# Fetching and putting back the expert rows of a mixture-of-experts layer by a fixed number for each place, instead of by whole groups of 32

## The chip, the cores and the metric

The kernel runs on one core of one Trainium2 chip. The metric is device time in microseconds (us), lower is better. The engines are named as in the profile: PE is TensorE (PEld its weight loads), DVE is VectorE, ACT is ScalarE, POOL is GpSimd, SP is SyncE. The core's 16 DMA engines move all data between HBM and the on-chip memory, whichever engine issues the transfer.

## The reference, cut to what matters

One layer over 512 tokens of width 1024: adaLN, a projection, a convolution and attention, and then a mixture of experts in float32. A router gives each token four of 32 experts; each expert multiplies its tokens' rows by a 1024 x 2048 and a 1024 x 1024 matrix.

```python
def moe_ffn(h, w_router, b_router, w_gate_up, b_gate_up, w_down, b_down):
    logits = jnp.dot(h, w_router, preferred_element_type=jnp.float32) + b_router.astype(jnp.float32)
    top_logit, top_idx = lax.top_k(logits, TOP_K)
    gate = jax.nn.softmax(top_logit, axis=-1)
...
    def expert_block(args):
        tok, g, e = args
        xb = h_pad[tok]
        gu = xb @ w_gate_up[e] + b_gate_up[e]
        y = clamped_swiglu(gu) @ w_down[e] + b_down[e]
        return y * g[:, None].astype(y.dtype)
...
    out = jnp.zeros((n_tok + 1, d), y.dtype).at[slot_tok].add(y.reshape(n_slots, d))
```

There are 512 x 4 = 2048 pairs of token and expert. How many fall to each expert depends on the data.

## The kernel before, in words

The first 330 us or so are the dense part (adaLN, projections, attention, convolution, output projection, router). The rest is the experts.

**Places.** The kernel counts the tokens of each expert on the chip and sorts the experts by count (`sort`). Expert 0 always has place 0; the others have places 1 to 31, by falling count. The numbers of slots are fixed for each place: 128 for places 0 to 3, 96 for places 4 to 15, 64 for places 16 to 31, that is `groups(i)` groups of `W = 32`, 2688 slots in all. `idx` holds, for each place, the token of each slot; an empty slot points to a spare row of its own, past the 512 tokens. Tokens that find no slot go to an `overflow` branch, which loads the weights of their expert once more. With the counts that the reference's inputs give (seeds 0 to 3), no expert has more tokens than its place has slots.

**Order of work.** The places are worked off in the order of `place(i)`, i from 0 to 31: a place of the upper half (four or three groups, called heavy here) and one of the lower half (two groups, light) in turn. For each expert there are eight loads of 1 MB for the first product and four for the second. `fetch` issues them from SP, in one order written out ahead (`seq`), into a ring of 1 MB buffers: 13, and 6 more from the sixth product of expert 0 on. A load waits until PE has read its buffer, and until the load eight places ahead, whose semaphore it takes over, has landed; so at most eight loads are under way.

**Rows.** `gather(i)` (POOL, an indirect DMA from the DRAM table `H2` into `xg`) fetches n rows of 4 KB, one a partition; `turn_x(i)` transposes them on PE. `gather(i + 2)` is issued as soon as `turn_x(i + 1)` has freed `xg`. `put_back(i)` weighs the products on DVE into `y`, and `scatter` (POOL, an indirect DMA) adds the n rows of `y` to the DRAM table `ACC`. Place 0 isn't fetched (it is built on the chip) and place 31 isn't put back (its rows are added on the chip), so 31 transfers of either kind run. The matrix products always work on whole groups.

## Time and profile before

| | us |
|---|---|
| time, median of 3 runs (1430.43 to 1435.80) | 1435.26 |
| the profiled execution: its own time | 1430.19 |
| its span, first to last instruction | 1428.5 |
| PE busy with matmuls | 1303.4 |
| DVE busy | 470.3 |
| POOL busy | 193.4 |

The profiled execution's time is its span and 1.7 us around it. It is as fast as the fastest of the three runs and 5.1 us under their median. A busy PE is not a PE at its peak: matmul records overlap and their ends are modelled.

### The profile page before, as it was taken

The numbers are of one execution on the slowest core, as the hardware profiler recorded it, in microseconds if no ns is written. First come the engines' busy times: TensorE is split into PE (matmuls) and PEld (weight loads), VectorE is DVE, ScalarE is ACT, GpSimd is POOL, SyncE is SP. The second block draws the span as 40 slices with busy tenths as digits, with TensorE's granted clock in tenths as the row PEclk, the third lists the DMA queues.
The fourth block names the chain that finished last, engine by engine and source line by source line (L and its number), as shares of the span: only waits on it lengthen the run. The fifth ranks groups of instructions, "written<-read, shape, count | busy, mean of one in ns | idle before, by whom it ended". The sixth has DMA issues, their size and how long they took to land.

```text
span 1428.5 us, 29373 instructions
## 1 busy us (share of the span) xinstructions
PE 1303.4 (91%) x12798; PEld 645.1 (45%) x12798; DVE 470.3 (33%) x954; ACT 227.7 (16%) x362; POOL 193.4 (14%) x152
## 2 busy tenths in 40 slices
PE   5799879998899999999989899998989899989894
PEld 1577768784444343444434333433333344434341
DVE  2787655546122331222222121322121222131224
ACT  1425555432000010000000000000000000000002
POOL 0421632212002100000010000010000000000102
PEclk9899999999999999999999999999999999999997
DMA  9446524237999999999999999999999999999994
GB/s 351 165 156 228 206 91 165 99 125 289 378 381 372 394 399 399 397 402 396 402 397 399 393 414 395 407 380 391 401 395 412 396 399 394 397 395 392 397 393 183
DMA packets 79486, 483.05 MB, mean 338 GB/s; under 512 B 9725, under 2 KB 10553, under 8 KB 27129
## 3 DMA queue, kind: packets, MB, share of 16 engines
q1 hardware_dynamic: 71298, 453.58, 79.7%
q0 software_dynamic: 7952, 27.53, 7.3%
q8 instruction: 102, 1.67, 0.5%
q14 instruction: 30, 0.25, 0.0%
q10 hardware_dynamic: 104, 0.03, 0.0%
HBM read 463.01 MB, written 18.09 MB: 337 GB/s over the span
## 4 chain that ended last, share of the span: by engine, by line
DMA 36%; PE 34%; issue 2%; DVE 1%; ACT 1%; ACTq 0%; SPq 0%; DVEq 0%
DMA raw<-in_w_gate_up_dram 19%; PE R L1013 11%; PE S L1013 9%; DMA hl<-in_w_gate_up_dram 8%; PE J L1013 7%; DMA hl<-in_w_down_dram 6%; DMA raw<-in_w_down_dram 3%; PE V L1013 3%; PE S L1256 1%; PE S L1027 1%; PE T L1220 1%; PE V L1038 1%; ACT aT L1267 0%; PE R L1027 0%; PE T L1256 0%
## 5 line engine op out<-in xcount | busy, mean ns | idle before, releaser
L1013 PE MATMUL S<-raw,xT 128*32 128x512 f32 x1440 | 174.3, 601 | 15.6 <-DMA raw<-in_w_gate_up_dram 13.9
L1013 PE MATMUL J<-raw,xT 128*32 128x512 f32 x1424 | 165.0, 595 | 7.5 <-DMA raw<-in_w_gate_up_dram 7.2
L1286 DVE SCALAR_TENSOR_TENSOR y<-R,gates,gt2r 32x256 f32<-32x256 f32 x208 | 99.9, 480 | 209.5 <-PE R L1013 206.7
L1270 POOL DMA_INDIRECT ACC<-y,idx x31 | 45.3, 1463 | 798.8 <-DVE selx L1060 798.8
L1286 DVE SCALAR_TENSOR_TENSOR y<-V,gates,gt2r 32x256 f32<-32x256 f32 x120 | 57.5, 479 | 240.6 <-PE V L1013 239.1
L1225 ACT ACTIVATE xT<-T 128x512 f32<-128x512 f32 (+1 forms) x31 | 18.2, 587 | 640.4 <-PE T L1220 599.9
L1013 PE MATMUL R<-raw,aT 128*32 128x256 f32 x2144 | 118.0, 379 | 2.4 <-DMA raw<-in_w_down_dram 2.4
L1013 PE MATMUL R<-raw,xT 128*32 128x512 f32 x896 | 114.1, 598 | 0.0
L1013 PEld LDWEIGHTS R<-raw,aT 128*32 128x32 f32 x2144 | 74.5, 110 | 48.9 <-PE J L1013 6.8
L1013 PEld LDWEIGHTS S<-raw,xT 128*32 128x32 f32 x1440 | 42.4, 110 | 107.5 <-issue 69.9
L1013 PEld LDWEIGHTS J<-raw,xT 128*32 128x32 f32 x1424 | 41.6, 109 | 101.4 <-issue 73.7
L1013 PE MATMUL V<-raw,aT 128*32 128x256 f32 x1280 | 73.6, 380 | 5.9 <-DMA raw<-in_w_down_dram 5.8
L1013 PE MATMUL S<-hl,xT 128*32 128x512 f32 x608 | 72.7, 595 | 6.8 <-DMA hl<-in_w_gate_up_dram 6.8
L1013 PE MATMUL J<-hl,xT 128*32 128x512 f32 x624 | 73.4, 596 | 4.4 <-DMA hl<-in_w_gate_up_dram 4.3
L1237 DVE TENSOR_SCALAR lm<-S 128x512 f32<-128x512 f32 x16 | 11.1, 692 | 196.7 <-ACT sg L1236 196.7
L1013 PE MATMUL R<-hl,aT 128*32 128x256 f32 x1184 | 67.7, 386 | 1.4 <-DMA hl<-in_w_down_dram 1.4
L1013 PEld LDWEIGHTS R<-raw,xT 128*32 128x32 f32 x896 | 30.8, 112 | 67.3 <-issue 67.2
L1013 PEld LDWEIGHTS V<-raw,aT 128*32 128x32 f32 x1280 | 40.2, 110 | 41.7 <-DMA raw<-in_w_down_dram 12.4
L1013 PEld LDWEIGHTS R<-hl,aT 128*32 128x32 f32 x1184 | 39.5, 112 | 29.7 <-issue 4.2
L1206 POOL DMA_INDIRECT xg<-H,idx x31 | 29.2, 942 | 156.0 <-PE T L1220 87.5
L1013 PE MATMUL R<-hl,xT 128*32 128x512 f32 x384 | 48.3, 592 | 0.0
L519 POOL TENSOR_TENSOR acc<-acc,raw 128x2048 f32<-128x2048 f32 x8 | 37.4, 4669 | 51.3 <-ACT raw L518 51.2
(489 smaller groups left out, 1603.5 us busy)
## 6 DMA issues: line engine op xcount, KB each, us to landing
raw<-in_w_gate_up_dram SPq DMA_DIRECT2D x179, 1024.0 KB
raw<-in_w_down_dram SPq DMA_DIRECT2D x85, 1024.0 KB
hl<-in_w_gate_up_dram SPq DMA_DIRECT2D x77, 1024.0 KB
hl<-in_w_down_dram SPq DMA_DIRECT2D x43, 1024.0 KB
raw<-in_w_ada_dram SPq DMA_DIRECT2D x24, 1024.0 KB
raw<-in_w_in_dram SPq DMA_DIRECT2D x10, 1024.0 KB
raw<-in_w_out_dram SPq DMA_DIRECT2D x4, 1024.0 KB
H<-t POOLq DMA_DIRECT2D x5, 512.0 KB, 3.2
```

Of the source, the lines that this page charges most:

```text
L519: G.tensor_add(v, v, t)
L1013: T.matmul(o(g)[j * W:(j + 1) * W], lhs(g), w(j), start=start and g % per == 0, stop=stop and (g % per == per - 1 or g == n - 1), skip_gro ...
L1027: T.matmul(a[g // 2][:, g % 2, :], selx[:, 2 * h:2 * h + 2, :].rearrange("p a c -> p (a c)"), bias[:, h * 512:(h + 1) * 512], start=False, ...
L1038: T.matmul(dn[i][n * HALF:(n + 1) * HALF, :], aT[i][:, r * 4 + j, :], w[:, r * D + n * 512:r * D + (n + 1) * 512], start=start, stop=stop)
L1206: G.indirect_dma_start(out=t, out_offset=None, in_=H2[:, :], in_offset=bass.IndirectOffsetOnAxis(ap=idx[0:n, q:q + 1], axis=0))
L1220: T.transpose(p_[:, c0:c0 + n], t[:, k * P:(k + 1) * P], ident[0:n, 0:n])
L1225: S.activation(d_, p_[:, 0:len(ks) * n], AF.Copy)
L1237: V.tensor_scalar(lv, u, LIMIT + 1.0, 1.0 - LIMIT, op0=OP.min, op1=OP.max)
L1256: T.transpose(p_[:, (2 * g + r) * P:(2 * g + r + 1) * P], r_[:, g * 256 + r:g * 256 + 256:2], ident)
L1270: G.indirect_dma_start(out=to, out_offset=bass.IndirectOffsetOnAxis(ap=ix_, axis=0), in_=y, in_offset=None, compute_op=OP.add)
L1286: V.scalar_tensor_tensor(y[g * W:(g + 1) * W, cs], quarter(a, g)[ps], gates4[ps, g, q:q + 1], gt2r[ps, cs], op0=OP.mult, op1=OP.mult)
```

## The change

`ROWS` gives a number of rows for each place, at most the slots that the place had: 2396 in all instead of 2688. `gather` and `scatter` move that many rows. The products, the transposes and the weighing still work on the whole groups, so the rows of `xg` past the fetched ones must hold something finite: `xg` becomes one tile (`xrows`) that is cleared once and then used by all gathers. The test for overflow now compares a count with `ROWS`: a table `less` (128 less the rows, by place) is filled by 23 memsets on POOL at the start, and one more DVE instruction behind the sort picks each expert's value. The last place's 512 gate columns, `gt2l`, move into `xrows`. With the reference's inputs (seeds 0 to 3) no count is over its place's new number, so the overflow branch stays untaken.

```diff
+ROWS = (128, 128, 112, 104, 96, 94, 90, 86, 84, 82, 80, 78, 78, 76, 75, 72,
+        64, 64, 64, 62, 62, 60, 60, 58, 58, 56, 56, 56, 55, 48, 46, 64)
...
     places()
+    for q in range(E):
+        if q == 0 or ROWS[q] != ROWS[q - 1]:
+            G.memset(less[:, q:E], float(P - ROWS[q]))
...
+        V.scalar_tensor_tensor(junk_[0:E, :], perm[0:E, 0, :], 1.0, less[0:E, :], op0=OP.mult, op1=OP.mult,
+                               accum_out=less_of)
...
-            V.tensor_copy(nb[:, 0:1], cnt[0:E, :])
-            for s in STEPS:
-                V.tensor_scalar(nb[:, 1:2], at[0:E, :], float(s), float(W), op0=OP.is_ge, op1=OP.mult)
-                V.tensor_add(nb[:, 0:1], nb[:, 0:1], nb[:, 1:2])
+            V.tensor_add(nb[:, 0:1], cnt[0:E, :], less_of)
...
     def gather(i):
-        n = groups(i) * W
-        t = m2.tile([n, D], F32, name="xg")
         q = place(i)
-        G.indirect_dma_start(out=t, out_offset=None, in_=H2[:, :],
+        n = ROWS[q]
+        t = xrows
+        G.indirect_dma_start(out=t[0:n, :], out_offset=None, in_=H2[:, :],
                              in_offset=bass.IndirectOffsetOnAxis(ap=idx[0:n, q:q + 1], axis=0))
...
-        q, a, n = place(i), dn.pop(i), groups(i) * W
-        y = m1.tile([n, D], F32, name="y", bufs=2)
+        q, a, n = place(i), dn.pop(i), ROWS[place(i)]
+        y = m1.tile([groups(i) * W, D], F32, name="y", bufs=2)
...
-        scatter(y, idx[0:n, q:q + 1])
+        scatter(y[0:n, :], idx[0:n, q:q + 1])
...
+    xrows = m2.tile([P, D], F32, name="xg")
+    V.memset(xrows, 0.0)
     gather(1)
```

The order of the transfers does not change; their sizes do. On POOL, from the third gather on (`xg<-H` is a gather, `ACC<-y` a scatter; 640 is the table's height), there stood before:

```order
L1206 DMA xg<-H_804,idx 96x1024
L1270 DMA ACC<-y,idx 640x1024
L1206 DMA xg<-H_804,idx 64x1024
L1270 DMA ACC<-y,idx 640x1024
L1206 DMA xg<-H_804,idx 96x1024
L1270 DMA ACC<-y,idx 640x1024
L1206 DMA xg<-H_804,idx 64x1024
L1270 DMA ACC<-y,idx 640x1024
L1206 DMA xg<-H_804,idx 128x1024
```

And in the same place now:

```order
L1213 DMA xg<-H_828,idx 94x1024
L1277 DMA ACC<-y,idx 640x1024
L1213 DMA xg<-H_828,idx 64x1024
L1277 DMA ACC<-y,idx 640x1024
L1213 DMA xg<-H_828,idx 90x1024
L1277 DMA ACC<-y,idx 640x1024
L1213 DMA xg<-H_828,idx 62x1024
L1277 DMA ACC<-y,idx 640x1024
L1213 DMA xg<-H_828,idx 128x1024
```

Before, every transfer had 64, 96 or 128 rows; now only places 1, 4, 16, 17, 18 and 31 keep their number, and most new numbers are no multiple of 16. SP's queue is the same, row for row. At the program's start POOL gets the memsets ahead of the clearing of `c64`, the left operand of the first products (`c_183`); these are the last six of them:

```order
L323 MEMSET less 128x9
L323 MEMSET less 128x7
L323 MEMSET less 128x4
L323 MEMSET less 128x3
L323 MEMSET less 128x2
L323 MEMSET less 128x1
L364 MEMSET c_183 128x512
L365 COPY c_183<-sl 128x8x2
```

Before, the memset of `c64` followed that of `ones_bf` at once. All but the first of the 23 wait for the one ahead, as they overlap.

## Rows read from the trace of the kernel before

**Rows 1.** The page: span; DMA share in 40 slices, in tenths.

```profile
span 1428.5 us, 29373 instructions
DMA  9446524237999999999999999999999999999994
```

**Rows 2.** Chain that ended last, 330 to 1429 us: start, us, what.

```profile
604.40 6.91 PE V L1013 x128
...
642.21 21.33 DMA raw<-in_w_down_dram
663.66 23.65 DMA raw<-in_w_gate_up_dram
...
1351.18 20.83 DMA hl<-in_w_down_dram
```

**Rows 3.** Windows: length, busy PE, PEld, DVE, ACT, POOL, granted clock, DMA share, GB/s.

```profile
440.00:640.00 200.00, 197.01 (x2225) 82.43 (x2221) 49.31 (x97) 15.53 (x27) 18.91 (x18) 1.00 1.02 392
640.00:1380.00 740.00, 687.89 (x7863) 285.39 (x7859) 167.87 (x342) 44.18 (x79) 51.83 (x43) 1.00 1.02 398
```

**Rows 4.** SP's waits, 740 to 1040 us: total us, times, longest.

```profile
SPq L128 <- DMA raw<-in_w_gate_up_dram: 115.8, 49, 4.7
...
SPq L128 <- PE R L1013: 4.2, 13, 0.4
```

**Rows 5.** DMA, 740 to 1040 us: packets, MB, share of 16 engines' time.

```profile
DMA packets 17336, 119.59 MB, mean 399 GB/s; under 512 B 2011, under 2 KB 2011, under 8 KB 3515
...
q1 hardware_dynamic: 15514, 112.98, 92.8%
q0 software_dynamic: 1792, 6.16, 8.3%
```

**Rows 6.** DMA, 497 to 504 us, a scatter of 64 rows.

```profile
q1 hardware_dynamic: 338, 2.44, 83.8%
q0 software_dynamic: 80, 0.26, 18.8%
```

**Rows 7.** DMA, 504 to 512 us, a gather of 96 rows.

```profile
q0 software_dynamic: 112, 0.39, 15.3%
```

**Rows 8.** DMA, 563 to 570 us, a gather of 128 rows.

```profile
q0 software_dynamic: 144, 0.52, 18.3%
```

**Rows 9.** Timeline of POOL: start, us, idle before. Gathers of i = 1, 4, 6.

```profile
362.71 0.98 POOL L1206 DMA_INDIRECT xg<-H,idx  x1 [16.04 <-issue]
452.05 0.96 POOL L1206 DMA_INDIRECT xg<-H,idx  x1
501.32 0.93 POOL L1206 DMA_INDIRECT xg<-H,idx  x1 [5.49 <-PE T L1220]
```

**Rows 10.** Timeline of PE: transposes of the same rows, i = 4, 6.

```profile
470.66 0.63 PE L1220 MATMUL T<-ident,xg 96*128 96x96 f32 x5
529.87 0.63 PE L1220 MATMUL T<-ident,xg 96*128 96x96 f32 x5
```

**Rows 11.** Tile `xg`: the transposes (ns min/median/max, first and last start); the gathers' landing.

```profile
L1220 PE MATMUL T<-ident,xg x200: 222/223/329, 391.0 to 1362.0; 64*128 64x64 f32 x64, 96*128 96x96 f32 x30, 128*128 128x128 f32 x6
...
DMA to landing us min/median/max: 7.8/9.1/12.2
```

**Rows 12.** Timelines of POOL and PE at the start.

```profile
0.38 0.10 POOL L1556 MEMSET const-float32-0.0<- 128x1 f32 x1 [0.38 <-issue]
...
5.02 0.20 POOL L359 COPY c<-sl 128x16 f32<-128x16 f32 x1 [2.80 <-DVE sl L355]
...
6.64 1.93 PE L378 MATMUL S<-raw,c 128*32 128x512 f32 x8 [3.82 <-DMA raw<-in_w_ada_dram]
```

**Rows 13.** Timeline of DVE, the sort and what follows.

```profile
336.99 0.17 DVE L1071 SCALAR_TENSOR_TENSOR kj<-T,own 64x32 f32<-64x32 f32 x1
...
352.47 1.28 DVE L1132 SCALAR_TENSOR_TENSOR bias<-y,sgn 128x1024 fp32r<-128x1024 f32 x1 [1.12 <-ACT y L1131]
...
378.56 0.69 DVE L1237 TENSOR_SCALAR lm<-S 128x512 f32<-128x512 f32 x1 [18.80 <-ACT sg L1236]
```

## The prediction

> **What bounds the kernel now.** I read the page first. The 16 DMA engines are idle for a good part of the dense stage and busy to nine tenths or more in every slice from 357 us to the tail [rows 1]. Then the chain: up to 640 us it consists of PE's products, from 642 us to 1372 us of transfers, nearly without a break [rows 2]. The windows say the same: from 440 to 640 us PE is busy for 197 of 200 us, from 640 to 1380 us for 688 of 740, so it stands still for 52 us there. The granted clock is 1.00 in both, the upper of its two levels, and the DMA share is 1.02 in both [rows 3]. SP's waits show why the transfers don't run ahead: between 740 and 1040 us SP waits 115.8 us for the landing of earlier loads into the first product's buffers alone, and 4.2 us for PE to give a buffer back [rows 4]. So the eight loads under way are the limit, and the DMA engines are full all the time. What is taken from their work after 440 us shortens the end by as much, as long as that is less than the 52 us that PE has to spare.

> **What a row costs.** The gathers and scatters are queue q0, the weights q1. Between 740 and 1040 us q0 has 1792 packets: 9 gathers and 9 scatters with 16 small ones each (288), and 1504 rows. Its share is 8.3% of 16 x 300 us, so 398 us, or 0.265 us of one engine for a row [rows 5]. The kinds differ. A scatter of 64 rows takes 18.8% of 16 x 7 us, which is 21.1 us or 0.329 us a row [rows 6]; a gather of 96 rows 15.3% of 16 x 8 us, 19.6 us or 0.204 us a row [rows 7]; a gather of 128 rows 18.3% of 16 x 7 us, 20.5 us or 0.160 us a row [rows 8]. So the gather of 128 rows costs hardly more than that of 96: where the rows lie on the partitions matters, not only how many they are. I take 0.204 for all gathers that are not of 128 rows.

> **What is saved.** 31 gathers fetch 2560 rows before and 2268 after, 31 scatters put back 2624 and 2332: 292 fewer of each. The first places (16, 4, 17) keep their rows, so all of it falls after 440 us. Scatters: 292 x 0.329 = 96.1 us. Gathers: 252 of the rows belong to places that had 96 or 64, 252 x 0.204 = 51.4 us; places 2 and 3 go from 128 rows to 112 and 104, and so from 2 x 20.5 us to 216 x 0.204 = 44.1 us, 3.1 us more. In all 144.4 us of one engine.

> What that is worth depends on how the rows are dealt out to the engines. Every transfer of before has a multiple of 16 rows, so no row here shows what happens with 94, 62 or 55. From both sides:
> - The rows are dealt out evenly, whatever their number: 144.4 / 16 = 9.0 us. (By q0's mean, 584 x 0.265 / 16 = 9.7 us; by bytes alone, 2.39 MB at the window's 398 GB/s, 6.0 us.)
> - All 16 engines take blocks, and the number is rounded up: an engine has n / 16 rows, rounded up. Every load of weights needs all 16 engines, so the fullest one counts, and it is always the same. It saves a row only at places 2, 3, 10 to 15, 29 and 30, ten in each direction: scatters 10 x 0.329 = 3.3 us; gathers 8 x 0.204 less 2 x 0.15 (8 rows at 0.160 become 7 at 0.204), 1.3 us; in all 4.6 us.

> That the price of a gathered row depends on the number of rows speaks for blocks of neighbouring partitions for each engine, so I take 4.6 us, and keep 9.7 as the other end.

> **What is added.**
> - 23 memsets on POOL at the start. A small one takes 0.10 us [rows 12]; as each waits for the one ahead I allow up to 0.19, 2.3 to 4.4 us. The copy of the conditioning vector into `c64` stands behind them; it ran at 5.02 us after 2.80 us of idleness, and the first product that reads it began at 6.64 us, when its weights had landed [rows 12]. So POOL, free for the copy from 2.2 us before, is free from 4.5 to 6.6 us now; copy and product begin at most about 0.4 us late. I take 0.2. Without that idle time it would be the whole 4.4.
> - One DVE instruction behind the sort, on the way to the table of experts that SP waits for: the nearest one took 0.17 us [rows 13]. In front of the overflow test four small ones go. I take 0.2.
> - Clearing `xrows`: up to 1.3 us, from the widest DVE instruction near it [rows 13]. DVE stands idle for 18.8 us ahead of its next work [rows 13], so nothing behind it waits, but the first gather now waits for it. It was issued at 362.7 us [rows 9], lands within 12.2 us, and is first read at 391.0 [rows 11]: nothing. Without that cover, 1.3 us.

> The products, transposes and weighing don't change. One tile for all gathers instead of a new one each time changes no wait: the next gather waited before, too, until PE had read the last [rows 9, 10].

> **Sum.** 4.6 saved, 0.4 added: 4.2 us less. On the profiled execution, 1430.19 us, that is 1426.0. The median of the runs lies 5.07 us above that execution; a difference carries over, so I forecast 1435.3 - 4.2 = 1431 us, with a range of its own of 1425 (9.7 saved) to 1435 (nothing saved but the added 0.4 hidden).

> **Rivals.**

> *Few engines per transfer (slower).* A block split needs not be rounded up: the transfer could be given to as many engines as divide its number of rows, at most 16. All of before are multiples of 16, and their 16 small packets per transfer [rows 5] fit this as well. Then 94, 90 and 62 rows go to 2, 15 and 2 engines. Two engines serve places 5, 7, 9, 19, 20, 23, 24 and 30 (548 rows), both ways. The work is no more than in the even case, but one engine of such a pair gets 274 x (0.204 + 0.329) = 146 us over 16 transfers, or 18.3 us for each of the 16 engines on the average. The loads of weights run at the pace of the engine that is furthest behind; eight loads under way, 8.4 MB at 398 GB/s, let the others run ahead by 21 us and no more. If the pairs come round evenly, the fullest is over the mean by about one large scatter, 47 x 0.329 - 2 = 13 us; if each transfer begins at the engine after the last one's, the ones with 15 and 14 engines move the start back by one or two, and the put back rows of experts 9, 10 and 14 and the fetched ones of 14 and 15 meet on one engine: (31 + 43 + 41) x 0.329 + (41 + 29) x 0.204 = 52 us, 34 over the mean. So 9.0 less and 13 to 34 more: 1440 to 1460, and I take 1450. It costs more than it saves as soon as one engine is over the mean by 9 us. A second effect speaks for slower as well: the gather for i = 4 has only 18.6 us from its issue to its first transpose, where that for i = 6 has 28.6 [rows 9, 10]. Landing takes 9.1 us in the middle [rows 11] with six rows an engine; 41 more at 0.204 and, if the two queues take turns, a packet of weights between each (83.8% of 112 us over 2.44 MB of 8 KB packets, 0.315 us [rows 6]) make it 30 us, so PE would stand for about 12 us at 470 us. PE is 197 of 200 us busy there; but the DMA engines go on loading meanwhile, into buffers that are free.

> [...]

> *An even deal.* As above, 9.0 saved and 0.4 added: 1426.7 us. For it: nothing obliges a list of rows to be cut in blocks. Against it: the gather's price by number of rows.

> *Hidden anyway.* If PE were the bound over the whole expert stage, nothing would come of it: 1435 us. The chain speaks against it from 642 us on [rows 2], and PE's 52 idle us [rows 3].

> **How the numbers follow.** Chances: all 16 engines with rounding up (the forecast) 0.33 and evenly 0.20, together the likelier kind; few engines 0.42; hidden 0.05. About 0.5%, 7.2 us, is what a measurement of this kernel can tell from no change. Faster by more: 0.65 of the even deal, a quarter of the forecast's case, little of the others, 0.24. Slower by more: most of the few engines' case, 0.38. Within: 0.38. The range reaches down to the even deal with its upper price and 2 us for the spread of the runs, 1423, and up to 1458, which leaves out the last part of the few engines' case.

> **What would show it.** q0's packets fall by 584, and its share between 740 and 1040 us by about a tenth, in every case. Right: the gathers' median landing stays within 1 us of 9.1, rates in the windows stay near 398 GB/s, and the last load lands some 4 us earlier. Wrong: landings of 20 us and more for 94, 86 and 82 rows, rates that fall under 390 GB/s after 640 us, and PE waiting there for more than 52 us. If the chain in the middle turns into PE, the hidden case holds.

## The result, and the profile after

The changed kernel takes 1472.88 us (median of 4 runs, 1470.36 to 1477.46) against 1432.85 us before (4 runs); the ratio is 1.0268, 95% interval 1.0242 to 1.0295. With fewer rows it is 40 us slower. The forecast was 1431 us with a range up to 1458.

From the page of the kernel after (span; DMA share in 40 slices; queues with packets, MB, share of 16 engines' time):

```profile
span 1472.1 us, 29396 instructions
DMA  8445544148999999999998999999999999999983
q1 hardware_dynamic: 71298, 453.58, 78.9%
q0 software_dynamic: 15824, 25.19, 6.8%
```

And the two queues on the page of the kernel before:

```profile
q1 hardware_dynamic: 71298, 453.58, 79.7%
q0 software_dynamic: 7952, 27.53, 7.3%
```

q0 moved fewer bytes, but its packets doubled. Its engine time fell from 7.3% of 1428.5 us, 104.3 us, to 6.8% of 1472.1, 100.1 us. The weights on q1, the same packets and bytes as before, went from 79.7% or 1138.5 us to 78.9% or 1161.5 us: 23 us more. (A share is rounded to 0.1%, so each of these is good to 0.7 us.) Together the DMA engines have 18.8 us more to do, and the span is 43.6 us longer; the other 25 us the engines stood idle. (The profiled execution of before is one of the fast ones, so the spans lie a little further apart than the medians.)

Where they stood idle the windows show (length, busy PE, PEld, DVE, ACT, POOL, granted clock, DMA share, GB/s):

```profile
440.00:640.00 200.00, 175.94 (x1968) 73.48 (x1964) 41.78 (x83) 13.14 (x23) 22.46 (x22) 0.93 1.01 384
640.00:1380.00 740.00, 689.67 (x7760) 285.11 (x7756) 168.65 (x342) 43.36 (x77) 60.84 (x44) 0.99 1.00 381
...
640.00:740.00 100.00, 98.50 (x1160) 42.13 (x1156) 23.99 (x48) 6.25 (x11) 9.33 (x6) 1.00 1.02 388
740.00:840.00 100.00, 87.70 (x956) 34.69 (x948) 22.38 (x46) 5.62 (x10) 9.09 (x6) 0.96 0.93 335
```

Before, the share was 1.02 and the rate 392 and 398 GB/s [rows 3]; now it is 381 GB/s after 640 us, and 335 at a share of 0.93 in the worst stretch, 740 to 840 us. The mean granted clock fell to 0.93 between 440 and 640 us, where PE was busy for 176 us instead of 197. That is a mean of two levels, 1.00 and 0.50: in windows of 2 us the clock is 1.00 up to 476 us, 0.50 from 478 to 486 and 1.00 again from 488, and 0.50 from 578 to 592 us, each time after PE had stopped for rows that had not landed (no product runs from 476 to 482 and from 576 to 586 us). Between 480 and 500 us the mean is 0.80, between 580 and 600 us 0.66. In the kernel before the lower level, 0.50, shows from 1424 to 1428 us. The chain (start, us, what) has such waits at 455 and 547 us and is made of transfers from 690 us on, almost without a break, as it was from 642 us before [rows 2]:

```profile
455.40 27.69 DMA xg<-H,idx
...
690.05 23.50 DMA raw<-in_w_down_dram
...
757.57 35.57 DMA raw<-in_w_down_dram
```

Some 9 of the 25 idle us lie in the last 88.5 us of the span. The first line is the kernel before, the second the kernel after:

```profile
1340.00:1428.50 88.50, 65.73 (x676) 26.73 (x668) 28.75 (x67) 13.81 (x30) 13.29 (x13) 0.92 0.79 313
```

```profile
1383.50:1472.10 88.60, 62.72 (x568) 23.58 (x560) 28.69 (x67) 13.51 (x29) 13.88 (x13) 0.86 0.69 264
```

SP still waits for landings, not for buffers (740 to 1040 us; total, times, longest), as in [rows 4]:

```profile
SPq L130 <- DMA raw<-in_w_gate_up_dram: 110.8, 43, 4.8
...
SPq L130 <- PE R L1019: 1.8, 6, 0.4
```

**How many engines a transfer gets.** One scatter stands alone in its stretch, that of the 46 rows of place 30 (DMA, 1395 to 1412 us):

```profile
q1 hardware_dynamic: 810, 5.94, 86.2%
q0 software_dynamic: 384, 0.19, 6.7%
```

384 packets for 46 rows. If two engines carry 23 rows each, and the other 14 get an all but empty packet in each of the 23 turns, that is 46 + 23 x 14 = 368, and with the 16 of the end 384. The sizes in the trace say the same: 46 packets of 4 KB, 322 of 8 bytes and 16 of 4 bytes. Counted so for all transfers, with the largest divisor of the number of rows up to 16 as the number of engines, q0 should have 7952 of before, less 584 rows, and 8456 small packets more, 15824; the page has 15824. No packet's record names its engine: a number of engines means this count, here and below. The times of the records agree with it: of the 54 rows that the gather of 94 moved between 455 and 473 us no more than two were ever under way at once, of the 96-row gather of before up to 13. A turn is also long: the rows of the scatter of 46 follow one another from 1396.2 to 1409.3 us, so each of the 23 turns took some 0.6 us, of which the row itself is 0.33; the 64 rows of before, four on each engine, were done in less than 7 us [rows 6].

The first gather by two engines (i = 4) landed 27.7 us after its issue (chain above), and PE, with nothing else to do, waited 9 us for it (timelines of POOL and PE):

```profile
455.40 1.53 POOL L1213 DMA_INDIRECT xg<-H,idx  x1 [0.18 <-issue]
...
483.23 1.04 PE L1227 MATMUL T<-ident,xg 96*128 96x96 f32 x5 [8.96 <-DMA xg<-H,idx]
```

The wait table has all such waits (total us, times, longest), none of which was there before; a scatter must also wait for the one ahead of it to land, since both add to `ACC`:

```profile
POOL ACC L1277 <- DMA ACC<-y,idx: 87.4, 3, 30.7
...
PE T L1227 <- DMA xg<-H,idx: 25.6, 3, 12.9
```

**The weights' packets get longer** beside a gather. DMA of the kernel after, 460 to 480 us, with that gather and, from 473 us on, the scatter issued behind it:

```profile
q1 hardware_dynamic: 905, 6.59, 89.9%
q0 software_dynamic: 804, 0.54, 12.0%
```

DMA of the kernel before, 480 to 494 us, with hardly anything on q0:

```profile
q1 hardware_dynamic: 774, 5.65, 99.5%
...
q0 software_dynamic: 24, 0.03, 0.9%
```

A packet of 8 KB took 89.9% of 320 us / 804 = 0.358 us here, and 99.5% of 224 us / 690 = 0.323 us there. But the kernel before has longer packets, too. These are its gather of 96 rows (505 to 510 us) and its gather of 128 rows (564 to 569 us):

```profile
q1 hardware_dynamic: 176, 1.29, 76.8%
q0 software_dynamic: 112, 0.39, 24.6%
```

```profile
q1 hardware_dynamic: 225, 1.60, 75.9%
q0 software_dynamic: 144, 0.52, 25.7%
```

In the same way that is 0.390 us beside the gather of 96 rows, by 16 engines, and 0.311 us beside that of 128; beside the two-engine scatter of 46 rows (above) it is 0.323. With 112 rows by 16 engines it is 0.388 (multiples of 16, below, 829 to 834 us: 74.0% of 80 us, 1.25 MB). So it isn't the two engines that make the packets longer: in these traces gathers of 112 rows and fewer do, and those of 128 don't. On two engines such a gather lasts longer: that of 94 rows has its first packet at 460 us and lands at 483, where the 96 rows of before took from 505 to 510 us. So more packets of weights fall beside it.

### The profile page after: what moved, and what is told of

Read it like the earlier page. It is cut to its first block, busy times and chain, and to the rows that moved or that the text cites. A ratio compares the mean times of both kernels' runs of the same rounds, so it can differ in the third digit from the quotient of the medians.

```text
span 1472.1 us, 29396 instructions
## 1 busy us (share of the span) xinstructions
PE 1321.7 (90%) x12798; PEld 649.9 (44%) x12798; DVE 469.6 (32%) x953; ACT 228.0 (15%) x362; POOL 207.2 (14%) x175
## 3 DMA queue, kind: packets, MB, share of 16 engines
q1 hardware_dynamic: 71298, 453.58, 78.9%
q0 software_dynamic: 15824, 25.19, 6.8%
## 4 chain that ended last, share of the span: by engine, by line
DMA 50%; PE 20%; issue 2%; DVE 2%; ACT 0%; POOL 0%; ACTq 0%; SPq 0%; DVEq 0%; POOLq 0%
DMA raw<-in_w_gate_up_dram 20%; DMA raw<-in_w_down_dram 12%; DMA hl<-in_w_gate_up_dram 10%; PE R L1019 7%; PE S L1019 5%; DMA xg<-H,idx 5%; PE J L1019 4%; DMA hl<-in_w_down_dram 3%; PE V L1019 2%; DMA y<-in_b_down_dram 1%; DVE y L1293 1%; PE V L1044 1%; PE S L1263 0%; PE S L1033 0%; PE T L1227 0%
## 5 line engine op out<-in xcount | busy, mean ns | idle before, releaser
L1019 PE MATMUL S<-raw,xT 128*32 128x512 f32 x1440 | 180.0, 616 | 13.3 <-DMA raw<-in_w_gate_up_dram 11.1
L1277 POOL DMA_INDIRECT ACC<-y,idx x31 | 52.7, 1700 | 824.2 <-DVE selx L1067 736.8
L1019 PEld LDWEIGHTS R<-raw,aT 128*32 128x32 f32 x2144 | 70.9, 110 | 53.4 <-issue 7.7
L1213 POOL DMA_INDIRECT xg<-H,idx x31 | 33.0, 1065 | 159.2 <-PE T L1227 83.0
L1227 PE MATMUL T<-ident,xg 64*128 64x64 f32 (+2 forms) x200 | 22.1, 251 | 25.6 <-DMA xg<-H,idx 25.6
```

The lines of the kernel that those rows point to most:

```text
L1019: T.matmul(o(g)[j * W:(j + 1) * W], lhs(g), w(j), start=start and g % per == 0, stop=stop and (g % per == per - 1 or g == n - 1), skip_gro ...
L1213: G.indirect_dma_start(out=t[0:n, :], out_offset=None, in_=H2[:, :], in_offset=bass.IndirectOffsetOnAxis(ap=idx[0:n, q:q + 1], axis=0))
L1227: T.transpose(p_[:, c0:c0 + n], t[0:n, k * P:(k + 1) * P], ident[0:n, 0:n])
L1277: G.indirect_dma_start(out=to, out_offset=bass.IndirectOffsetOnAxis(ap=ix_, axis=0), in_=y, in_offset=None, compute_op=OP.add)
```

## The experiments

**All additions, old numbers.** The `ROWS` of the whole groups; `FILLS` makes the memsets as many as in the change:

```diff
+ROWS = (128, 128, 128, 128, 96, 96, 96, 96, 96, 96, 96, 96, 96, 96, 96, 96,
+        64, 64, 64, 64, 64, 64, 64, 64, 64, 64, 64, 64, 64, 64, 64, 64)
+FILLS = (2, 3, 4, 5, 6, 7, 8, 9, 10, 11, 13, 14, 15, 16, 19, 21, 23, 25, 28, 29, 30, 31)
...
-        if q == 0 or ROWS[q] != ROWS[q - 1]:
+        if q == 0 or q in FILLS:
```

> The changed kernel with the old numbers of rows (128, 96, 64), and with all that the change adds: 23 memsets, the instruction behind the sort, one cleared tile for all gathers. Few-engines theory (the loss comes from numbers of rows that only a few engines can share): no loss beyond the additions; in the changed kernel the sort begins 3.1 us later than before (340.0 for 336.9), so 0 to 4 us over the kernel before. Rival, the additions and the shared tile cost the 40 us: about 40 us over.

Measured: 1433.41 us against 1433.85; ratio 0.9996 (0.9984 to 1.0009). The additions cost nothing that can be measured. The later sort in the changed kernel's trace was not their doing: here the sort's first instruction ran at 336.44 us.

**Multiples of 16.**

```diff
+ROWS = (128, 128, 112, 112, 96, 96, 96, 96, 96, 96, 80, 80, 80, 80, 80, 80,
+        64, 64, 64, 64, 64, 64, 64, 64, 64, 64, 64, 64, 64, 48, 48, 64)
```

> The changed kernel with each number rounded up to a multiple of 16 (2528 rows). Few-engines theory: every transfer has all 16 engines; ten rows an engine are saved each way, 4.6 us less by the prediction's prices, with fewer memsets (6): 3 to 5 us under the kernel before. Rival, a shared tile or shorter transfers cost by themselves: over the kernel before by 10 us or more.

Measured: 1429.81 us; ratio 0.9974 (0.9961 to 0.9986), or 3.7 us less (2.0 to 5.6). The tile, the memsets and shorter transfers are harmless, and the price per row of the prediction (4.6 us) fits.

**Gathers alone, scatters alone.** One side of the change is put back to whole groups:

```diff
-        q, a, n = place(i), dn.pop(i), ROWS[place(i)]
+        q, a, n = place(i), dn.pop(i), groups(i) * W
```

> Gathers with the new numbers, scatters with whole groups. Few-engines theory, by work on the engines: a gathered row costs 0.204 us and a put back one 0.329, so the gathers make about 0.4 of the loss, 15 us, and the stalls of PE on late rows (25.6 us in the changed kernel, 0 before) all stay: 15 to 25 us over the kernel before. Rival, late rows for PE are the whole loss: 35 to 40 us over.

```diff
-        n = ROWS[q]
+        n = groups(i) * W
```

> Scatters with the new numbers, gathers with whole groups. Few-engines theory, by work: 0.6 of the loss, 20 to 25 us over the kernel before, without a stall of PE on rows. Rival, late rows for PE are the whole loss: within 5 us of the kernel before.

Measured: gathers alone 1451.06 us, ratio 1.0120 (1.0104 to 1.0136), 17 us; scatters alone 1447.24, ratio 1.0084 (1.0064 to 1.0103), 12 us. Neither is the whole, nor are both together. The scatters missed their range of 20 to 25 us: they cost less than their share of the rows' work, so work on the engines is not the only price; and the expectation that the scatters alone would stop PE nowhere was roughly met (one wait of 6.5 us). In the kernel with the gathers alone, the gather of 86 rows by two engines has q0 to itself from 646 to 669 us:

```profile
q1 hardware_dynamic: 1110, 8.09, 95.6%
q0 software_dynamic: 702, 0.35, 6.5%
```

A packet of weights takes 95.6% of 368 us / 988 = 0.356 us there, for 23 us.

**Only the numbers for 11 and more engines; only those for 2 or 4.**

```diff
+ROWS = (128, 128, 112, 104, 96, 96, 90, 96, 84, 96, 80, 78, 78, 80, 75, 72,
+        64, 64, 64, 64, 64, 60, 60, 64, 64, 56, 56, 56, 55, 48, 48, 64)
```

> Only the numbers that leave 2 or 4 engines are rounded up to a multiple of 16 (2444 rows in all); those for 11 to 15 engines stay (90, 84, 78, 75, 72, 60, 56, 55, 104). Few-engines theory: the fullest engine has 6.1 us less than before by the prices per row: 3 to 7 us under the kernel before, a little better than the multiples of 16. Rival, every number that is not a multiple of 16 costs: over the kernel before by 5 us or more.

```diff
+ROWS = (128, 128, 112, 112, 96, 94, 96, 86, 96, 82, 80, 80, 80, 76, 80, 80,
+        64, 64, 64, 62, 62, 64, 64, 58, 58, 64, 64, 64, 64, 48, 46, 64)
```

> The other half of the change: numbers for 2 or 4 engines stay (94, 86, 82, 62, 62, 58, 58, 46, 76), all others are rounded up (2480 rows). If each transfer begins at the engine behind the last one's, these now come round evenly, and the fullest engine has 0.6 us more than before instead of 19. Theory that loads pile up on single engines: 0 to 15 us over the kernel before, the late rows' stalls included. Rival, each such transfer costs by itself, wherever it falls: 35 to 40 us over, as the whole change.

Measured: eleven or more 1431.01 us, ratio 0.9978 (0.9963 to 0.9993), 3.2 us less and not to be told from the multiples of 16. In this kernel a number that is no multiple of 16 does not cost by itself. Two or four alone 1441.97 us, ratio 1.0057 (1.0036 to 1.0079): 8 us, not 40, though every two-engine transfer of the change is there, and PE waits even longer for rows (30.9 us in 4 waits, 25.6 in the change). So the numbers for 2 or 4 engines are needed for the loss, but most of it arises only when those for 11 to 15 engines stand between them, which cost nothing alone. The harm of such a transfer depends here on what stands between it and the next one.

**One place of 94.** As the first experiment, with 94 for 96 at place 5.

```diff
+ROWS = (128, 128, 128, 128, 96, 94, 96, 96, 96, 96, 96, 96, 96, 96, 96, 96,
```

> The old numbers, but 94 instead of 96 rows at place 5 alone: two rows fewer, one gather and one scatter by two engines each. Theory that the end follows the fullest engine: 47 x 0.329 = 15.5 us on one engine instead of 2 to 3, for good: about 12 us over the kernel before. Rival, the loads under way (21 us) swallow a single lag: 0 to 3 us over. A gather that lands late stops PE in either case.

Measured: 1436.43 us, ratio 1.0009 (0.9990 to 1.0028). The theory missed, the rival held: a lag that the prices per row put at some 12 us on two engines, and 17.0 us of waiting for rows on PE, leave 1 us behind, if anything (the interval is -1.4 to 4.0).

**Two tiles for the rows.**

```diff
-RING3 = 6
+RING3 = 5
...
-        t = xrows
+        t = xrows[i % 2]
...
-            if i + 2 < E:
-                gather(i + 2)
+            if i + 3 < E:
+                gather(i + 3)
```

> The change with two tiles for the gathered rows, so that a gather is issued one expert earlier, for one buffer fewer in the ring of loads (18 for 19). No row should be late for PE. Theory that the pile on one engine is the larger part: 15 to 25 us over the kernel before. Rival 1, the late rows are the loss: within 5 us of it. Rival 2, late rows cost nothing, as the loads go on meanwhile: 38 to 42 us over, as the change.

> The new numbers in the gathers alone, with two tiles for the rows, so that none is late for PE; the order of the gathers, and so the engines that they fall on, is as with one tile (17 us over the kernel before). Theory that late rows cost little, since the loads go on meanwhile: 13 to 18 us over. Rival, the late rows (9.3 us of waiting on PE with one tile) count in full: 5 to 9 us over.

Measured: the whole change with two tiles 1455.54 us, ratio 1.0152 (1.0131 to 1.0173); PE waits for no rows. That is 17 us better than the change; but the earlier gathers also change the order of the transfers, and so, with the assumed start, the engines on which they meet: by prices per row the fullest engine then has 5.9 us more than before instead of 19. The gathers alone with two tiles keep their order: 1450.49 us, ratio 1.0111 (1.0092 to 1.0129), within the interval of 1.0120 with one tile. Late rows cost about 1 us there, too little to be told from none. The mean granted clock of the span rose from 0.970 to 0.977 with it, so the clock that PE loses by waiting is not the loss there either. The ring with one buffer fewer was not tried by itself; SP's longest row of waits for PE to give a buffer back (440 to 1400 us) is 11.2 us in all with it (the change with two tiles) and 9.0 without (the change).

**Does the start turn, and does the load pile up?** Both kernels have 62 rows at places 19 to 30. If each transfer begins at the engine behind the last one's, the 14-engine transfers between them turn the start back in the first kernel by as much as the 62-row ones move it on, and in the second it moves on evenly:

```diff
+ROWS = (128, 126, 126, 126, 96, 96, 96, 96, 84, 84, 84, 84, 84, 84, 84, 84,
+        64, 64, 64, 62, 62, 62, 62, 62, 62, 62, 62, 62, 62, 62, 62, 64)
```

> Old numbers but 62 rows at places 19 to 30 (two engines each) and 126 or 84 rows (14 engines) at places 1 to 3 and 8 to 15 (2562 rows). If each transfer begins at the engine behind the last one's, two 14-engine transfers move the start back by 4 and two 2-engine ones forward by 4: from the thirteenth expert on nearly all the 62-row gathers meet on one pair of engines, and the scatters on another. By the prices per row the fullest engine then has 57 us more than before. Theory of the turning start and the pile: 35 to 60 us over the kernel before, and the DMA engines partly idle. Rival, a transfer's engines are always the same or drawn anew: like the next kernel, within 10 us of it.

```diff
+ROWS = (128, 128, 128, 128, 96, 96, 96, 96, 96, 96, 80, 80, 80, 80, 80, 80,
+        64, 64, 64, 62, 62, 62, 62, 62, 62, 62, 62, 62, 62, 62, 62, 64)
```

> The same 62 rows at places 19 to 30, but multiples of 16 (128, 96, 80) at all other places (2568 rows), so that the start moves on by two engines with each 62-row transfer and the load comes round evenly; the fullest engine has 1.8 us more than before. Theory of the turning start and the pile: 3 to 15 us over the kernel before, and the DMA engines full. Rival, as for the kernel ahead of it: no difference between the two.

Measured: piled up 1500.68 us, ratio 1.0463 (1.0445 to 1.0481); evenly 1454.58 us, ratio 1.0139 (1.0121 to 1.0158). The two-engine transfers are the same; 84 rows, by 14 engines, were among the numbers that cost nothing above (1431.01 us); yet 46 us lie between, where the prices per row and the assumed start put 55 between the fullest engines. With engines that are always the same, or drawn anew, the two should have been about alike. Both are over their ranges (66 us where 35 to 60, 20 where 3 to 15 were expected). No packet's record names its engine, so the turning start stays an assumption that this difference fits; and 126 rows were not tried without the 62. The windows from 1200 to 1300 us, piled up:

```profile
1200.00:1300.00 100.00, 87.13 (x935) 36.25 (x928) 21.00 (x42) 5.65 (x10) 9.18 (x6) 0.98 0.95 345
```

and evenly:

```profile
1200.00:1300.00 100.00, 92.55 (x1092) 39.94 (x1084) 24.30 (x50) 5.62 (x10) 8.76 (x6) 1.00 1.02 382
```

Piled up, the DMA engines are idle as in the changed kernel between 740 and 840 us; evenly, they are full and yet move 382 GB/s. The queues of the even kernel, on its page, show why it is 20 us slower all the same, more than was expected:

```profile
span 1455.8 us, 29379 instructions
...
q1 hardware_dynamic: 71298, 453.58, 79.4%
q0 software_dynamic: 18128, 26.61, 7.2%
```

The same weights take 1155.9 us, 17.4 more than before. That is the longer packet again, and it is most of what the even kernel loses: its span is 27.3 us over that of before, its median 20. In the piled up kernel the weights take 78.0% of 1500.8 us, 1170.6, or 32 more. So of the 45 us between these two spans some 15 are longer packets, 3 are q0's, and some 27 are idle engines: half of what the totals of the fullest engines gave.

**The fewest turns.** Each number is raised to the next that 14 to 16 engines share in equal parts:

```diff
+ROWS = (128, 128, 112, 105, 96, 96, 90, 90, 84, 84, 80, 80, 80, 80, 75, 75,
+        64, 64, 64, 64, 64, 60, 60, 60, 60, 56, 56, 56, 56, 48, 48, 64)
```

> Each number raised to the next one that 14 to 16 engines can share in equal parts with the fewest rows an engine (2427 in all): 105, 96, 96, 90, 90, 84, 84, 80, 80, 80, 80, 75, 75 for the heavy places from 3 on, 64, 60, 56 and 48 for the light ones. Few-engines theory: all engines nearly even, rows saved as with the multiples of 16 or a little more: 3 to 7 us under the kernel before.

Measured: 1426.94 us against 1434.28; ratio 0.9949 (0.9931 to 0.9967), 7.3 us less (4.7 to 9.9), at the upper end of its range. It beats both kernels. Its page:

```profile
span 1425.7 us, 29386 instructions
...
q1 hardware_dynamic: 71298, 453.58, 79.9%
q0 software_dynamic: 7632, 25.39, 6.7%
```

The weights are back at 1139.1 us, and q0 takes 95.5 us, 8.8 less than before.

## Why the prediction was wrong

- **What bounds the kernel**: right. The chain is transfers, SP waits for landings, and where the weights' rate fell the time rose.
- **The price of a row** fits. 4.6 us were forecast for rows dealt to all engines, rounded up; the multiples of 16, which are just that, gave 3.7, and the fewest turns 7.3, near the even deal's 9.0.
- **The step that failed** is the one from the gather's price to the deal: "That the price of a gathered row depends on the number of rows speaks for blocks of neighbouring partitions for each engine, so I take 4.6 us". Blocks there may be, but nothing in that row says how many engines get one; that where the rows lie on the partitions matters, inferred from 19.6 us for 96 rows and 20.5 for 128, no run shows either. The packets were counted with the largest divisor up to 16 as the number of engines, and the pages agree exactly: 15824 in the change, 18128 in the even kernel, 7632 with the fewest turns. "q0's packets fall by 584 ... in every case" was wrong with it: they doubled. The rival *few engines*, with a chance of 0.42, was the case. The divisor is that of the transfer's own number of rows; with the table's 640 rows counted in as the other side, 90 rows would get 10 engines instead of 15, and the change 19696 packets instead of 15824. All 16 engines with the rows rounded up would have left the change 7368 packets.
- **The signs**: of those named for "wrong", late landings came (27.7 us for 94 rows, 40.1 at the most) and rates under 390 GB/s after 640 us (381). PE standing for more than 52 us there did not (50.3).
- **The rival was mis-sized**: 1450 with 1460 at its end, against 1472.9. Its 13 to 34 us for the pile rest on which engines the transfers get, which no run shows; the runs show 8 us for the two- and four-engine transfers alone, 40 for the whole change and 46 between piled up and evenly. An estimate with the assumed start fits them: with all transfers counted at the prices per row, the fullest engine has 104.7 us of rows instead of 85.5, 19 more where the rival's upper end, with its rows on one engine, came to 25; engines stand idle from 740 to 840 us (share 0.93), where with that start the puts of experts 9 and 10 meet. "The work is no more than in the even case" was wrong: a gather on two engines lasts longer (23 us where 5 were enough), so more of the weights' packets beside it are long; they take 23 us more of every engine in the change, 15 with the gathers alone. 23 of longer packets, 4 less on q0 and 25 of idleness make the 43.6 us between the spans. That the 25 are all the pile's is not shown: 9 of them are in the last 88.5 us, and the change with two tiles has by that estimate only 5.9 us more on its fullest engine but some 15 us more of idleness (79.3% and 6.9% of 1457.4 us on the two queues). The estimated total of the fullest engine alone doesn't give the time: with one place of 94 it is 12 us over, too, and nothing measurable is lost (ratio 1.0009).
- **The single lag** that is not made good: the rival was worked with the fullest engine's total, on the reasoning that the loads run at the pace of the engine furthest behind. That every load needs all 16 engines is read from its 16 small packets (1723 of q1's under 512 B for 107.7 loads [rows 5]); no run shows that pace: with one place of 94 a lag estimated at 12 us left 1 us behind, if anything. That only loads which meet within a short stretch let the others run dry fits the piled up kernel and is not shown otherwise. Where the swallowed lag goes is open.
- **The late gather**: right in size (30 us forecast, 27.7 measured; 12 us of waiting, 9.0), and right that the loads go on meanwhile: in the gathers alone it costs too little to measure. What it costs in the whole change beside the pile is not separated.
- **The additions**: 0.4 us forecast; -0.6, between -2.3 and 1.3, measured.

Why a gather of 112 rows or fewer makes the weights' packets longer (0.390 and 0.388 us, against 0.311 beside 128 rows) is not settled. The gathers alone (79.6% of 1449.4 us on the weights, 15 us more than before) do more of it than the scatters alone (79.2% of 1446.9, 7 us more), where the gathers still have whole groups but come behind two-engine scatters.

## What to carry to other kernels

In these runs it paid to choose the number of rows of an indirect transfer by its divisors: numbers that 14 to 16 engines share in equal parts took 1426.94 us, multiples of 16 alone 1429.81, while 94 or 62 rows were dealt to two engines by the packet count. One place of 94 was not felt (1436.43 us, ratio 1.0009), but 62 rows instead of 64 at twelve places made the kernel 20 us slower, and 66 with 84 and 126 rows at eleven of the other places. Where a transfer's size is new to the trace, count the packets on its queue after the first run: here 15824 instead of the 7368 expected told how the rows were dealt. A cost that is put on "the transfer itself" should also be looked for in the other queue's packets: the same 71298 packets of weights took 23 us longer on every engine, for the larger part beside gathers that lasted longer.

## What was not expected of the hardware

Beside its rows a transfer by two engines has hundreds of packets of 4 or 8 bytes, as many as if each engine without a row in a turn got one: the scatter of 46 rows is 384 packets, one of 64 rows 80 [rows 6]. What was issued behind a scatter of 94 rows in the kernel after began only when the scatter's small packets were nearly through: the gather of 62 rows issued at 547.03 us, 2.9 us behind that scatter, landed after 40 us, as the chain shows:

```profile
547.03 40.09 DMA xg<-H,idx
```

The small packets of the two differ in size, so the trace shows this. The scatter's 658 of 8 bytes run from 549.98 to 564.64 us; the gather's first, of 4 bytes, comes at 562.97, 16 us after its issue. The scatter lands at 579 us, the gather's last rows begin before 580, but its small packets go on to 586.7. That these last ones belong to the two engines that had been busy with the scatter's rows is the author's reading; no run shows it by itself. And one late gather and one scatter of 94 rows on two engines cost too little to be told from nothing (ratio 1.0009), while the two-engine transfers of the whole change, among the others, go with 40 us.
